# A hybrid decoder trunk on one core: output weight sums moved to VectorE in quarter pieces, and an opening without GpSimd

## The chip, the cores and the metric

The kernel runs on one core of a Trainium2 chip. The metric is device time in microseconds. Three runs of the kernel before took 1044.41, 1044.99 and 1047.21 us; the median is 1044.99. The core has five engines with a queue of instructions each: TensorE (PE in the rows, PEld for its weight loads), VectorE (DVE), ScalarE (ACT), GpSimd (POOL) and SyncE (SP), which here only issues DMAs. Each engine works its queue in order.

## The reference

One layer over 1056 tokens (1024 prompt tokens and 8 samples of 4), model width 1024, all in float32:

```python
n = rmsnorm(h, g_in)
proj = n @ w_in                  # z_a | xBC (x 1024, B 256, C 256) | dt 16 | z_b | u_b
ya = ssd_branch(z_a, xbc, dt)    # causal conv (width 4) + SiLU, chunked SSD scan, gate, grouped norm
yb = s5_branch(u_b, z_b)         # diagonal complex scan, gelu, GLU, gate
h = h + concat(ya, yb) @ w_out
gate = sigmoid(rmsnorm(h, g_ple) @ w_ple_gate)
h = h + (p @ w_ple_proj) * gate
y = rmsnorm(h, g_final)
```

The outputs are y and the new convolution, SSD and S5 states.

## The kernel before

Tokens stand on the free axis in three chunks of 352 columns, channels on the 128 partitions. Every float32 product is made of three matmuls: a weight block and the activations are each split into a rounded high part (ScalarE copies it) and a low part (VectorE subtracts), and high x high, high x low and low x high are summed in PSUM. One projection tile (`dense`) is 3 chunks x 8 blocks of K x 3 = 72 matmuls.

The stages, in the order of the code:

- **Opening.** PE multiplies zeros (`zp`), then the tiles of p @ w_ple_proj (`pp_tile` 0 to 7, 18 matmuls each, inputs `p_h`, `p_l`). Beside it the input norm is made for each of the three chunks: `norm_sum` (ScalarE squares the eight blocks of x into `xsq`, seven adds collect them in `xsa`), `norm_tok` (PE sums over partitions into `nsp`; then twelve tiny VectorE instructions on 88 x 4 values, `nv`, `ny`, `nt`, make the reciprocal root), `norm_apply` (PE spreads the root to all partitions, `nrb`; VectorE scales the eight blocks of x, and each is split into `n_h` and `n_l`). The adds of chunk 0 are VectorE's, those of chunks 1 and 2 GpSimd's; of chunk 1 GpSimd also makes three of the eight `n_l`.
- **First tiles and S5 coefficients.** Tiles u0, z0 and u1 are computed chunk by chunk, and the norms of chunks 1 and 2 are put between their matmuls by the table `mids`. Then VectorE works out the S5 coefficients (`s5_coef_base`, `s5_coef_batch`) while PE does the other u tiles; PE transposes their results (`wp`).
- **Middle (`MID`).** Seventeen tiles: twelve convolution tiles (`conv_tile`: 72 matmuls, then three long VectorE instructions into `acc`), four z tiles, one small `dt` tile. Behind each tile but the first stands one of 16 S5 batches (`s5_batch`): PE makes `vr` and `vi`, VectorE turns, scans and turns back into `sst`, PE makes the output `yp` from `sst`.
- **SSD**, in 16 units, with the other z tiles among them; then the GLU, then w_out, then gate and final norm.

The product with w_out is made of 7 block products instead of 8 (Strassen's scheme). It needs four sums of weight blocks, s1 to s4. `wo_sums` makes them: for each of 4 blocks i it loads a21, a22, a11, a12 (two DMAs of 128 x 512 each) into row buffers `wa` of 1024 columns, makes four GpSimd instructions of 128 x 1024, and stores each sum to `ws_d` in DRAM. They are read there much later. The code asks for two sums behind each of `MID`'s tiles 1 to 8.

What sets the order: a scheduler of the framework lays out every engine's queue from modelled times, by readiness and by the order of the code, so an instruction may be placed well before where the code has it. `tc.issue_after` (here `behind`) makes it place an instruction after another one. Loads and stores of SP stand in one queue: a store that waits for its data holds all that is behind it. Row buffers come from one pool of 28.

Of the kernel before, what the change touches and what calls it, by code (L numbers as in the profile page):

```python
# [26 lines left out]
WSUM = {i: 2 for i in range(1, 9)}  # L27
# [5 lines left out]
V_GIN, V_CW, V_CB, V_NG, V_GLUB, V_GPLE, V_GFIN = 0, 8, 56, 68, 76, 84, 92  # L33
C_CAUS, C_ONE, C_SMASK, C_BM, C_E8, C_I32, C_SAME, C_E16, C_ID, C_N = 0, 128, 256, 288, 296, 360, 392, 424, 440, 568
# [3 lines left out]
def hymba_ssd_s5_kernel(  # L38
# [29 lines left out]
    NSUM, NSPL = (V, G, G), ((), (1, 3, 5), ())  # L68
# [95 lines left out]
    WO_SUM = ("s1", "s2", "s3", "s4")  # L164
# [7 lines left out]
    def wo_sums():  # L172

        for i in range(4):
            a = {}
            for n, o, x, y, op, ld in (("s1", "a22", "a21", "a22", ALU.add, ("a21", "a22")),
                                       ("s3", "a21", "a11", "a21", ALU.subtract, ("a11",)),
                                       ("s2", "a11", "a22", "a11", ALU.subtract, ()),
                                       ("s4", "a12", "a12", "a11", ALU.subtract, ("a12",))):
                for blk in ld:  # L180
                    a[blk] = row("wa")[:, 0:1024]
                    for q, src in enumerate(wo_src(blk, i)):
                        dma(out=a[blk][:, 512 * q:512 * q + 512], in_=src)
                tt(a[o], a[x], a[y], op, G)
                dma(out=ws_d[WO_SUM.index(n), i], in_=a[o])
                yield
# [29 lines left out]
    def dense(w, rows_h, rows_l, evac, K=8, ko=0, chunks=((0, CW), (CW, CW), (2 * CW, CW)), ps_of=lambda c: psd_(),  # L216
              after=None, mid=None):
        hi, lo = w
        chained = after is not None
        for c, (t0, n) in enumerate(chunks):  # L220
            ps = ps_of(c)[:, 0:n]
            i = 0
            for k in range(K):
                if mid and k == mid[0]:
                    pe_end[0] = after
                    mid[1]()
                    after = pe_end[0]
# [23 lines left out]
    pe_end, v_end = [None], [None]  # L251
# [82 lines left out]
    for i in range(8):  # L334
        pe_end[0] = PE.matmul(out=zp[:, 0:128], lhsT=z0, rhs=z0, start=True, stop=True)
# [17 lines left out]
    def pp_tile(m, w):  # L353
        o = pet("pe", F32) if m in PEP else cvt("pe")

        def evac(c, t0, n, ps):
            if c == 1:
                ts(o[:, t0:t0 + n], ps, 0.5, None, ALU.mult)
            else:
                act(o[:, t0:t0 + n], ps, scale=0.5)  # L360
        pe_end[0] = dense(w, p_h, p_l, evac, K=2, ko=2 * (m % 4), ps_of=lambda c: psb("psd") if c == 2 else psd_(),
                          after=pe_end[0])
        dms(out=pp_d[m], in_=o[:, 0:T])

    def norm_sum(c):
# [3 lines left out]
        for k in range(1, 8):  # L369
            sq = ev("xsq")  # L370
            act(sq, x[k], AF.Square)
            add(sa, sa, sq, NSUM[c])
# [5 lines left out]
    def norm_apply(c, y):  # L378
        x = [xr[k][:, c * CW:c * CW + CW] for k in range(8)]
        rs = rstd_bcast(y, pe_end[0])  # L380
        for k in range(8):
            stt(x[k], x[k], vc[:, V_GIN + k:V_GIN + k + 1], rs, ALU.mult, ALU.mult)
            end = split(n_h[k][:, c * CW:c * CW + CW], n_l[k][:, c * CW:c * CW + CW], x[k],
                        G if k in NSPL[c] else V)
# [9 lines left out]
    n_end = norm_apply(0, y0)  # L394
# [3 lines left out]
    sa1 = norm_sum(1)  # L398
    pp_tile(4, w_pp2)
    pp_tile(5, w_pp2)  # L400
    w_u0 = split_w(r_u0)
    y1 = norm_tok(sa1)
    pp_tile(6, w_pp2)
    pp_tile(7, w_pp2)
    with behind(n_end):
        w_z0 = split_w(r_z0, [row(n, F32R)[:, 0:1024] for n in ("zwh", "zwl")])
    w_u1 = load_w(M_U + 1)
# [214 lines left out]
    def conv_tile(m, name):  # L622
# [16 lines left out]
        for k in (2, 1, 0):  # L639
            stt(acc[:, 0:1080], raw[:, k:k + 1080], cw(k), acc[:, 0:1080], ALU.mult, ALU.add)  # L640
# [81 lines left out]
    def z_evac(j):  # L722
        dst = zb_d[j] if j < 8 else za_d[j - 8]

        def evac(c, t0, n, ps):
            t = ev("zt", n)
            if j >= 8:
                act(t, ps, AF.Tanh, scale=0.5)
                stt(t, t, 1.0, ps, ALU.add, ALU.mult)
# [4 lines left out]
            for a, b, d0, ns in ((0, nn, 0, 8),) + (((nn, n, NPT, 4),) if nn < n else ()):  # L734
# [3 lines left out]
                stt(v, v, 1.0, pv, ALU.add, ALU.mult)  # L738
# [283 lines left out]
    later = {}  # L1022

    def norm2():
        later["y"] = norm_tok(norm_sum(2))

    def norm_end():
        later["end"] = norm_apply(2, later["y"])

    mids = {(0, 0): (3, lambda: norm_apply(1, y1)), (0, 1): (0, norm2), (1, 0): (0, norm_end)}  # L1030
    for c in range(3):
        for i, (w, e) in enumerate(first):
            pe_end[0] = dense(w, n_h, n_l, lambda _, t0, n, ps: e(c, t0, n, ps), chunks=((CW * c, CW),), after=pe_end[0],
                              mid=mids.get((c, i)))
    n_end = later["end"]
# [13 lines left out]
    nb, sums = 0, wo_sums()  # L1049
    for i, nm in enumerate(MID):  # L1050
# [345 lines left out]
```

## Time and profile before

| | |
|---|---|
| Median of 3 runs | 1044.99 us |
| The profiled execution | 1044.09 us, its span 1042.3 us |
| PE busy | 995.8 us (96% of the span) |
| DVE busy | 814.2 us (78%) |
| ACT busy | 454.4 us (44%) |
| POOL busy | 222.5 us (21%) |

The profile gives for one execution the start and duration of every instruction, what ended an engine's idle time, and PE's granted clock. PE is the engine that is nearly always busy. So the time moves with PE's idle stretches, with the stretches in which its clock is granted at half (1.2 instead of 2.4 GHz), and with the number of its matmuls. Matmuls overlap: what one costs is the distance from its start to the next start, not its duration. The same holds for VectorE's instructions.

### The profile page before, as it was taken

To read this page: it belongs to the slowest core of one execution; us is meant where nothing else is said; L and a number is where in the kernel's file an instruction comes from. 1 tells how busy PE (TensorE), PEld (TensorE's weight loads), DVE (VectorE), ACT (ScalarE), POOL (GpSimd) and SP (SyncE) were. 2 spreads that over 40 slices of the span, in tenths; PEclk is the share of its full clock that TensorE was granted. 3 is DMA by queue.
4 is the path that set the end of the run, shared out by engine and by line. 5 is a ranking of instruction groups with operands and counts; after the bars stand their busy time and mean duration, and the time that the engine had idled before them with its cause. 6 is when DMAs were issued, how large, how long until landed. Compare 5 with 4: busy or idle time off the path is not lost.

```text
span 1042.3 us, 19520 instructions
## 1 busy us (share of the span) xinstructions
PE 995.8 (96%) x7148; PEld 942.8 (90%) x7148; DVE 814.2 (78%) x1804; ACT 454.4 (44%) x1006; POOL 222.5 (21%) x215
## 2 busy tenths in 40 slices
PE   7999999997899999999999998899999999899995
PEld 6999989986799999999878887799999999899995
DVE  5888999776989887873866777868688879977466
ACT  6532233344245353445764445244345445454221
POOL 2401030025500000001243323121232015541221
PEclk8899999998999999999999999999999999999998
DMA  9426599886855644545456667576544323335122
GB/s 343 162 67 200 154 275 259 210 276 247 240 187 153 196 113 129 168 141 151 132 180 199 201 191 214 161 208 166 166 120 134 110 88 118 112 124 171 48 94 104
DMA packets 170832, 174.88 MB, mean 168 GB/s; under 512 B 47728, under 2 KB 129136, under 8 KB 170736
## 3 DMA queue, kind: packets, MB, share of 16 engines
q1 hardware_dynamic: 140704, 153.23, 48.6%
q10 hardware_dynamic: 30032, 20.40, 6.2%
q8 instruction: 56, 0.92, 0.4%
q14 instruction: 40, 0.33, 0.1%
HBM read 123.05 MB, written 54.73 MB: 171 GB/s over the span
## 4 chain that ended last, share of the span: by engine, by line
PE 67%; DVE 17%; DMA 7%; issue 4%; ACT 3%; SPq 0%; POOL 0%; DVEq 0%; ACTq 0%
PE psd L231 43%; PE psd L1204 12%; PE yp L306 3%; DVE wl L77 2%; DVE rb L77 2%; PE nrb L290 1%; DVE acc L89 1%; DMA gr<-gd 1%; PE yd L860 1%; DMA ab<-acs_d 1%; PE st L912 1%; ACT ab L74 1%; DVE x L89 1%; ACT wh L74 1%; DVE opn L77 1%
## 5 line engine op out<-in xcount | busy, mean ns | idle before, releaser
L231 PE MATMUL psd<-n_h,wh 128*128 128x352 f32 x840 | 275.1, 327 | 0.0
L231 PE MATMUL psd<-n_l,wh 128*128 128x352 f32 x840 | 274.5, 327 | 0.0
L231 PE MATMUL psd<-n_h,wl 128*128 128x352 f32 x840 | 273.8, 326 | 0.0
L231 PEld LDWEIGHTS psd<-n_h,wh 128*128 128x128 f32 x840 | 158.1, 188 | 10.0 <-issue 9.8
L1204 PE MATMUL psd<-opn,wh 128*128 128x264 f32 x896 | 164.0, 285 | 0.0
L231 PEld LDWEIGHTS psd<-n_h,wl 128*128 128x128 f32 x840 | 158.3, 188 | 3.1 <-issue 2.6
L231 PEld LDWEIGHTS psd<-n_l,wh 128*128 128x128 f32 x840 | 158.2, 188 | 2.8 <-issue 2.5
L1204 PEld LDWEIGHTS psd<-opn,wh 128*128 128x128 f32 x896 | 138.6, 188 | 0.1
L1204 PE MATMUL psd<-opn,wl 128*128 128x264 f32 x448 | 126.9, 285 | 3.6 <-DVE wl L77 3.6
L74 ACT ACTIVATE wh<-wr 128x512 fp32r<-128x512 f32 x147 | 85.7, 623 | 94.3 <-PE psd L231 38.1
L77 DVE TENSOR_TENSOR wl<-wr,wh 128x512 fp32r<-128x512 f32 x146 | 106.9, 758 | 24.4 <-ACT wh L74 23.5
L1204 PEld LDWEIGHTS psd<-opn,wl 128*128 128x128 f32 x448 | 84.2, 188 | 4.2 <-DVE wl L77 4.2
L77 POOL TENSOR_TENSOR wa<-wa 128x1024 f32<-128x1024 f32 x16 | 44.2, 2761 | 121.7 <-DMA wa<-wall 111.3
L74 ACT ACTIVATE ab<-ab,tok 128x128 f32<-128x128 f32 (+1 forms) x144 | 42.8, 379 | 53.3 <-DMA ab<-acs_d 40.7
L231 PE MATMUL psd<-g_h,wh 128*128 128x384 f32 (+1 forms) x168 | 54.1, 322 | 0.1
L231 PE MATMUL psd<-g_l,wh 128*128 128x384 f32 (+1 forms) x168 | 54.0, 321 | 0.0
L231 PE MATMUL psd<-g_h,wl 128*128 128x384 f32 (+1 forms) x168 | 53.9, 321 | 0.0
L77 POOL TENSOR_TENSOR xl<-xl,h 128x264 f32<-128x264 f32 x32 | 29.7, 933 | 87.9 <-DVE h L77 34.7
L231 PE MATMUL psd<-hg_h,gwl 128*128 128x400 f32 (+1 forms) x144 | 46.6, 324 | 0.0
L231 PE MATMUL psd<-hg_h,gwh 128*128 128x400 f32 (+1 forms) x144 | 46.5, 323 | 0.0
L231 PE MATMUL psd<-hg_l,gwh 128*128 128x400 f32 (+1 forms) x144 | 46.4, 323 | 0.0
L74 ACT ACT_TABLE_LOAD x29 | 37.2, 1283 | 19.2 <-DVE acc L89 11.1
(323 smaller groups left out, 2079.0 us busy)
## 6 DMA issues: line engine op xcount, KB each, us to landing
wr<-wall SPq DMA_DIRECT2D x128, 256.0 KB, 3.4
wa<-wall SPq DMA_DIRECT2D x32, 256.0 KB, 6.1
ws_d<-wa SPq DMA_DIRECT2D x16, 512.0 KB, 5.5
mm<-md SPq DMA_DIRECT2D x16, 512.0 KB, 5.3
ab<-acs_d SPq DMA_DIRECT2D x16, 512.0 KB, 5.2
wr<-ws_d SPq DMA_DIRECT2D x32, 256.0 KB, 2.9
ud<-ub ACTq DMA_DIRECT2D x8, 576.0 KB, 4.7
u<-ud SPq DMA_DIRECT2D x16, 288.0 KB, 4.1
```

The costliest lines, as they stand in the source:

```text
L74: return S.activation(out=out, in_=in_, func=func, **kw)
L77: return (eng or V).tensor_tensor(out=out, in0=a, in1=b, op=op)
L89: return V.scalar_tensor_tensor(out=out, in0=a, scalar=s, in1=b, op0=op0, op1=op1)
L231: end = PE.matmul(out=ps, lhsT=a[:, ko + k, :], rhs=b, start=(i == 0), stop=(i == 3 * K - 1))
L290: end = PE.matmul(out=rb[:, qt * j:qt * j + qt], lhsT=y[:, j:j + 1].to_broadcast([qt, 128]), rhs=ident[0:qt, 0:qt], start=True, stop=True)
L306: self.last = f(*a, **kw)
L860: PE.matmul(out=yd[64 * (e % 2):64 * (e % 2) + 64, e // 2], lhsT=x1[:, e], rhs=mt[:, e], start=True, stop=True)
L912: PE.matmul(out=st, lhsT=bk, rhs=x2.rearrange("p e q -> p (e q)"), start=True, stop=True)
L1204: PE.matmul(out=ps, lhsT=a[:, k, :], rhs=b, start=(k == 0 and q == 0), stop=(k == 7 and q == 2))
```

## The change

- **Sums.** `wo_sums(n)` now works on a quarter: 256 columns of each of the four blocks in one row buffer, loaded by two DMAs (128 x 2 x 256, so pieces of 1 KB where they were 2 KB), four VectorE instructions of 128 x 256 in place, one store of 512 KB in pieces of 1 KB. There are 16 such quarters, so 64 VectorE instructions in place of 16 GpSimd ones. Each is placed behind the last long VectorE instruction (`v_mid`) of its tile, at tiles 4 to 13 of `MID`, one or two a tile.
- **Opening.** All adds and all `n_l` are VectorE's; GpSimd has no part in it. The adds of chunk 1 are placed behind the root of chunk 0 and ahead of its scalings, those of chunk 2 behind the root of chunk 1 and ahead of its scalings. `mids` puts the norms later between the first tiles: chunk 1 is scaled behind u0 of chunk 0 (before: inside it), chunk 2 behind u0 of chunk 1 (before: ahead of it). VectorE's part in emptying PSUM of pp tiles 4 to 7 goes to ScalarE.
- **Zeros.** One more zero product at the start, and 4, 8 and 2 between the first matmuls of pp tile 0 (`ZER`).

```diff
@@ -26,3 +26,3 @@
 HT, CQ = 528, 264
-WSUM = {i: 2 for i in range(1, 9)}
+WSUM = {4: 1, 5: 2, 6: 1, 7: 2, 8: 1, 9: 2, 10: 2, 11: 2, 12: 2, 13: 1}
 PCH = ((0, 384), (384, 384), (768, 288))
@@ -33,2 +33,3 @@
 V_GIN, V_CW, V_CB, V_NG, V_GLUB, V_GPLE, V_GFIN = 0, 8, 56, 68, 76, 84, 92
+ZER = {(0, 1): 4, (1, 0): 8, (1, 1): 2}
 C_CAUS, C_ONE, C_SMASK, C_BM, C_E8, C_I32, C_SAME, C_E16, C_ID, C_N = 0, 128, 256, 288, 296, 360, 392, 424, 440, 568
@@ -67,3 +68,3 @@
     V, S, G, PE = nc.vector, nc.scalar, nc.gpsimd, nc.tensor
-    NSUM, NSPL = (V, G, G), ((), (1, 3, 5), ())
+    
 
@@ -163,3 +164,3 @@
     WO_BLK = dict(a11=(0, 0), a12=(0, 512), a21=(4, 0), a22=(4, 512))
-    WO_SUM = ("s1", "s2", "s3", "s4")
+    WO_SUM = ("s2", "s4", "s3", "s1")
 
@@ -171,17 +172,15 @@
 
-    def wo_sums():
+    def wo_sums(n):
 
-        for i in range(4):
-            a = {}
-            for n, o, x, y, op, ld in (("s1", "a22", "a21", "a22", ALU.add, ("a21", "a22")),
-                                       ("s3", "a21", "a11", "a21", ALU.subtract, ("a11",)),
-                                       ("s2", "a11", "a22", "a11", ALU.subtract, ()),
-                                       ("s4", "a12", "a12", "a11", ALU.subtract, ("a12",))):
-                for blk in ld:
-                    a[blk] = row("wa")[:, 0:1024]
-                    for q, src in enumerate(wo_src(blk, i)):
-                        dma(out=a[blk][:, 512 * q:512 * q + 512], in_=src)
-                tt(a[o], a[x], a[y], op, G)
-                dma(out=ws_d[WO_SUM.index(n), i], in_=a[o])
-                yield
+        i, q = n // 4, n % 4
+        base, o = (M_WOA, M_WOB)[q // 2] + i, 256 * (q % 2)
+        a = row("wa")[:, 0:1024].rearrange("p (m h c) -> p m h c", m=2, h=2)
+        for m in range(2):
+            dma(out=a[:, m], in_=wall[base + 4 * m].rearrange("p (h c) -> p h c", h=2)[:, :, o:o + 256])
+        a11, a12, a21, a22 = (a[:, j // 2, j % 2] for j in range(4))
+        add(a22, a21, a22)
+        sub(a21, a11, a21)
+        sub(a11, a22, a11)
+        sub(a12, a12, a11)
+        dma(out=ws_d[:, i, :, 256 * q:256 * q + 256].rearrange("s p c -> p s c"), in_=a.rearrange("p m h c -> p (m h) c"))
 
@@ -216,3 +215,3 @@
     def dense(w, rows_h, rows_l, evac, K=8, ko=0, chunks=((0, CW), (CW, CW), (2 * CW, CW)), ps_of=lambda c: psd_(),
-              after=None, mid=None):
+              after=None, mid=()):
         hi, lo = w
@@ -223,6 +222,7 @@
             for k in range(K):
-                if mid and k == mid[0]:
-                    pe_end[0] = after
-                    mid[1]()
-                    after = pe_end[0]
+                for k_, f in mid:
+                    if (c, k) == k_ if isinstance(k_, tuple) else k == k_:
+                        pe_end[0] = after
+                        f()
+                        after = pe_end[0]
                 h, l = rows_h[k][:, t0:t0 + n], rows_l[k][:, t0:t0 + n]
...
@@ -333,4 +333,9 @@
     zp = psa("zp")
-    for i in range(8):
-        pe_end[0] = PE.matmul(out=zp[:, 0:128], lhsT=z0, rhs=z0, start=True, stop=True)
+
+    def zeros(n):
+        for _ in range(n):
+            with behind(pe_end[0]):
+                pe_end[0] = PE.matmul(out=zp[:, 0:128], lhsT=z0, rhs=z0, start=True, stop=True)
+
+    zeros(9)
     for (t0, t1), (a, b) in zip(PS, WS):
@@ -356,3 +361,3 @@
         def evac(c, t0, n, ps):
-            if c == 1:
+            if c == 1 and m < 4:
                 ts(o[:, t0:t0 + n], ps, 0.5, None, ALU.mult)
@@ -361,3 +366,3 @@
         pe_end[0] = dense(w, p_h, p_l, evac, K=2, ko=2 * (m % 4), ps_of=lambda c: psb("psd") if c == 2 else psd_(),
-                          after=pe_end[0])
+                          after=pe_end[0], mid=[(q, lambda n=n: zeros(n)) for q, n in ZER.items()] if m == 0 else ())
         dms(out=pp_d[m], in_=o[:, 0:T])
@@ -371,3 +376,3 @@
             act(sq, x[k], AF.Square)
-            add(sa, sa, sq, NSUM[c])
+            s_end[0] = add(sa, sa, sq)
         return sa
@@ -382,4 +387,3 @@
             stt(x[k], x[k], vc[:, V_GIN + k:V_GIN + k + 1], rs, ALU.mult, ALU.mult)
-            end = split(n_h[k][:, c * CW:c * CW + CW], n_l[k][:, c * CW:c * CW + CW], x[k],
-                        G if k in NSPL[c] else V)
+            end = split(n_h[k][:, c * CW:c * CW + CW], n_l[k][:, c * CW:c * CW + CW], x[k])
         return end
@@ -393,3 +397,6 @@
     pp_tile(3, w_pp)
-    n_end = norm_apply(0, y0)
+    with behind(v_end[0]):
+        sa1 = norm_sum(1)
+    with behind(s_end[0]):
+        n_end = [norm_apply(0, y0)]
     r_z0 = load_raw(M_ZB)
@@ -397,12 +404,12 @@
         dma(out=xr[k][:, 2 * CW:T], in_=xT[k, :, 2 * CW:T])
-    sa1 = norm_sum(1)
     pp_tile(4, w_pp2)
-    pp_tile(5, w_pp2)
-    w_u0 = split_w(r_u0)
     y1 = norm_tok(sa1)
-    pp_tile(6, w_pp2)
-    pp_tile(7, w_pp2)
-    with behind(n_end):
+    for m in range(5, 8):
+        pp_tile(m, w_pp2)
+    with behind(n_end[0]):
+        w_u0 = split_w(r_u0)
         w_z0 = split_w(r_z0, [row(n, F32R)[:, 0:1024] for n in ("zwh", "zwl")])
-    w_u1 = load_w(M_U + 1)
+        with behind(v_end[0]):
+            sa2 = norm_sum(2)
+        w_u1 = load_w(M_U + 1)
     pe_es.close()
@@ -639,3 +646,3 @@
         for k in (2, 1, 0):
-            stt(acc[:, 0:1080], raw[:, k:k + 1080], cw(k), acc[:, 0:1080], ALU.mult, ALU.add)
+            v_mid[0] = stt(acc[:, 0:1080], raw[:, k:k + 1080], cw(k), acc[:, 0:1080], ALU.mult, ALU.add)
         act(cso[:, m, 0:3], raw[:, 1024:1027])
@@ -728,3 +735,3 @@
                 act(t, ps, AF.Tanh, scale=0.5)
-                stt(t, t, 1.0, ps, ALU.add, ALU.mult)
+                v_mid[0] = stt(t, t, 1.0, ps, ALU.add, ALU.mult)
                 dma(out=dst[:, t0:t0 + n], in_=t)
...
@@ -1021,11 +1028,14 @@
     first = ((w_u0, u_tile(0)), (w_z0, z_evac(0)), (w_u1, u_tile(1)))
-    later = {}
+    ny = {1: y1}
 
-    def norm2():
-        later["y"] = norm_tok(norm_sum(2))
+    def norm_a():
+        ny[2] = norm_tok(sa2)
 
-    def norm_end():
-        later["end"] = norm_apply(2, later["y"])
+    def norm_b(c):
+        def f():
+            with behind(s_end[0] if c == 1 else None):
+                n_end.append(norm_apply(c, ny[c]))
+        return f
 
-    mids = {(0, 0): (3, lambda: norm_apply(1, y1)), (0, 1): (0, norm2), (1, 0): (0, norm_end)}
+    mids = {(0, 1): [(0, norm_b(1))], (0, 2): [(1, norm_a)], (1, 1): [(0, norm_b(2))]}
     for c in range(3):
@@ -1033,4 +1043,4 @@
             pe_end[0] = dense(w, n_h, n_l, lambda _, t0, n, ps: e(c, t0, n, ps), chunks=((CW * c, CW),), after=pe_end[0],
-                              mid=mids.get((c, i)))
-    n_end = later["end"]
+                              mid=mids.get((c, i), ()))
+    n_end = n_end[2]
     with tc.issue_after(n_end.ins):
@@ -1048,3 +1058,3 @@
     s5c_["p1"] = pool("s51", 1, s5_es)
-    nb, sums = 0, wo_sums()
+    nb = nw = 0
     for i, nm in enumerate(MID):
@@ -1056,2 +1066,6 @@
             {"b": bt, "c": ct, "x": xs}[nm[0]][int(nm[1])] = conv_tile(CONV[nm], nm)
+        for _ in range(WSUM.get(i, 0)):
+            with behind(v_mid[0]):
+                wo_sums(nw)
+            nw += 1
         if i > 0 and nb < 16:
@@ -1059,4 +1073,2 @@
             nb += 1
-        for _ in range(WSUM.get(i, 0)):
-            next(sums)
     dma(out=o_conv, in_=cso)
...
```

Three places show how the queues change. First VectorE in the opening, from the end of chunk 0's root (`ny`) on; `wl` is the low part of a weight, `x_100` to `x_107` are the blocks of x. Before:

```order
L77 TENSOR_TENSOR nt<-nv,ny 88x4
L89 SCALAR_TENSOR_TENSOR nt<-ny,nt 88x4
L89 SCALAR_TENSOR_TENSOR ny<-nt,ny 88x4
L77 TENSOR_TENSOR wl<-wr,wh 128x512
L89 SCALAR_TENSOR_TENSOR x_100<-x_100,vc,nrb 128x352
```

And in the changed kernel, the same place in VectorE's queue:

```order
L78 TENSOR_TENSOR nt<-nv,ny 88x4
L90 SCALAR_TENSOR_TENSOR nt<-ny,nt 88x4
L90 SCALAR_TENSOR_TENSOR ny<-nt,ny 88x4
L78 TENSOR_TENSOR xsa<-xsa,xsq 128x352 x7
L90 SCALAR_TENSOR_TENSOR x_100<-x_100,vc,nrb 128x352
```

Seven adds of chunk 1 now stand between the root and the scalings; the weight's split has gone behind them.

Second, VectorE in a convolution tile of `MID` (tile 5, x1) in the changed kernel; `acc` is the convolution, `ta`, `tb`, `ur`, `ui` and `sst` are S5, `wa` the sums:

```order
L90 SCALAR_TENSOR_TENSOR acc<-x_3358,vc,acc 128x1080
L78 TENSOR_TENSOR wa<-wa 128x256 x2
L78 TENSOR_TENSOR sr<-sst 128x256
L78 TENSOR_TENSOR ta<-vi,cr 128x256
L78 TENSOR_TENSOR tb<-vr,sr 128x256
L78 TENSOR_TENSOR a4h<-a4h,vr 128x16
L78 TENSOR_TENSOR a4h<-a4h,vi 128x16
L822 SCALAR_TENSOR_TENSOR ur<-mag_609,ur 128x128 x2
L78 TENSOR_TENSOR wa<-wa 128x256 x2
L78 TENSOR_TENSOR ui<-ta,tb 128x256
L78 TENSOR_TENSOR wa<-wa 128x256 x2
```

Before, no sum stood in VectorE's queue; eight (two quarters) now stand among this tile's S5 work.

Third, PE at the end of the middle: `yp` is the output of the last S5 batch, `cb` and `xt` the first step of SSD, `psd` the matmuls of a z tile. Before:

```order
L231 MATMUL psd<-n_h_117,wl 128x352
L303 MATMUL yp<-sst,om 128x136
L306 MATMUL yp<-sst,om 128x136 x7
L306 MATMUL yp<-u_5373,mm 128x136 x4
L891 MATMUL cb<-c_2642,b_2541 128x128
L892 MATMUL cb<-ident_r,b_2541 128x128
```

And in the changed kernel:

```order
L231 MATMUL psd<-n_h_117,wl 128x352
L303 MATMUL yp<-sst,om 128x136
L306 MATMUL yp<-sst,om 128x136 x7
L306 MATMUL yp<-u_5436,mm 128x136 x4
L231 MATMUL psd<-n_h_110,wh 128x352
L231 MATMUL psd<-n_l_118,wh 128x352
```

The last `yp` stands 72 matmuls of z tiles behind the last convolution tile before, 120 in the changed kernel; the first `cb` and `xt` have gone ahead of it, and the first output of SSD (`yd`) comes 50 z matmuls later than before.

## Rows read from the trace of the kernel before

**Rows 1.** The page, part 1: busy time of each engine

```profile
PE 995.8 (96%) x7148; PEld 942.8 (90%) x7148; DVE 814.2 (78%) x1804; ACT 454.4 (44%) x1006; POOL 222.5 (21%) x215
```

**Rows 2.** Timeline of PE: start, us, instruction, count, idle time before it and releaser

```profile
0.99 3.78 PE L335 MATMUL zp<-zero 128*128 128x128 f32 x16 [0.99 <-POOL zero L332]
...
19.74 0.72 PE L268 MATMUL nsp<-cs,xsa 128*88 128x1 f32 x8
26.73 2.01 PE L290 MATMUL nrb<-ident_r,ny 88*128 88x88 f32 x8 [3.28 <-DVE ny L89]
...
37.30 0.32 PE L231 MATMUL psd<-p_l,wh 128*128 128x352 f32 x1
37.46 0.32 PE L231 MATMUL psd<-p_h,wl 128*128 128x352 f32 x1
...
44.95 1.12 PE L290 MATMUL nrb<-ident_r,ny 88*128 88x88 f32 x8 [0.94 <-DVE ny L89]
...
145.35 0.33 PE L303 MATMUL wp<-ident_r,wt 128*128 128x128 f32 x1 [2.17 <-DVE wt L77]
...
242.43 0.59 PE L303 MATMUL yp<-sst,om 64*128 64x136 f32 x1 [7.02 <-DVE sst L77]
...
281.14 0.41 PE L303 MATMUL yp<-sst,om 64*128 64x136 f32 x1 [4.92 <-DVE sst L77]
```

**Rows 3.** Windows: stretch, length, busy us of each engine, PE clock, DMA share, GB/s

```profile
300.00:480.00 180.00, 179.83 (x1354) 170.35 (x1353) 149.71 (x364) 86.97 (x180) 0.00 (x0) 1.00 0.49 143
480.00:500.00 20.00, 18.48 (x126) 17.51 (x125) 6.19 (x11) 13.42 (x37) 4.58 (x12) 1.00 0.49 139
...
8.00:16.00 8.00, 7.13 (x25) 6.58 (x26) 5.84 (x10) 6.21 (x14) 0.36 (x4) 0.57 1.05 386
26.00:32.00 6.00, 5.27 (x20) 5.27 (x21) 4.50 (x9) 1.90 (x5) 1.13 (x2) 0.50 0.39 141
240.00:248.00 8.00, 5.57 (x32) 5.32 (x32) 4.88 (x10) 4.84 (x7) 1.16 (x1) 0.55 0.60 174
280.00:288.00 8.00, 6.86 (x44) 6.62 (x45) 7.93 (x23) 2.73 (x6) 3.21 (x2) 0.79 0.75 224
```

**Rows 4.** Timeline of DVE in the opening

```profile
20.69 0.75 DVE L93 TENSOR_SCALAR ny<-nv 88x4 int32<-88x4 int32 x1
...
28.78 4.03 DVE L89 SCALAR_TENSOR_TENSOR x<-x,vc,nrb 128x352 f32<-128x352 f32 x8 [1.50 <-PE nrb L290]
...
54.54 0.16 DVE L93 TENSOR_SCALAR ny<-nv 88x4 int32<-88x4 int32 x1
...
62.09 3.56 DVE L77 TENSOR_TENSOR n_l<-x,n_h 128x352 fp32r<-128x352 f32 x8
```

**Rows 5.** Timeline of POOL

```profile
19.45 6.07 POOL L77 TENSOR_TENSOR xsa<-xsa,xsq 128x352 f32<-128x352 f32 x6 [8.75 <-ACT xsq L74]
...
230.92 10.24 POOL L77 TENSOR_TENSOR wa<-wa 128x1024 f32<-128x1024 f32 x4 [1.68 <-DMA wa<-wall]
```

**Rows 6.** Timeline of DVE in the middle

```profile
236.52 2.44 DVE L77 TENSOR_TENSOR ta<-ui,cr 128x256 f32<-128x256 f32 x1
238.88 2.56 DVE L77 TENSOR_TENSOR tb<-ur,sr 128x256 f32<-128x256 f32 x1
...
281.40 0.41 DVE L77 TENSOR_TENSOR ta<-vr,cr 128x256 f32<-128x256 f32 x1
281.74 0.41 DVE L77 TENSOR_TENSOR tb<-vi,sr 128x256 f32<-128x256 f32 x1
```

**Rows 7.** Instructions that write `wa`: shortest, median, longest ns; first and last start

```profile
L77 POOL TENSOR_TENSOR wa<-wa x16: 2402/2569/5372, 96.2 to 280.9; 128x1024 f32<-128x1024 f32 x16
```

**Rows 8.** Waits of DVE from 300 to 480 us

```profile
DVE tb L77 <- PE vi L306: 12.9, 9, 1.9
DVE sst L77 <- PE yp L306: 8.5, 3, 4.2
```

**Rows 9.** Waits of SP's queue

```profile
SPq L185 <- POOL wa L77: 8.9, 2, 8.3
```

More of the change, by code (lines that the diff above doesn't have):

```diff
@@ L250, in hymba_ssd_s5_kernel @@
     nw_p = pool("nw", bufs=2)
-    pe_end, v_end = [None], [None]
+    pe_end, v_end, v_mid, s_end = [None], [None], [None], [None]
     def rstd(sqs, n):
@@ L737, in evac @@
                 act(v, pv, AF.Tanh, scale=0.5)
-                stt(v, v, 1.0, pv, ALU.add, ALU.mult)
+                v_mid[0] = stt(v, v, 1.0, pv, ALU.add, ALU.mult)
                 o = dst[:, 0:NPT] if d0 == 0 else dst[:, NPT:T]
@@ L1085, in hymba_ssd_s5_kernel @@
             z_next()
-    assert nz[0] == 16
+    assert nz[0] == 16 and nw == 16
     glb = const.tile([128, 8], F32, name="glb")
```

## The prediction

> **What bounds the kernel now.** I began with the page's busy times: PE works 96% of the span, no other engine more than 78% [rows 1]. So I looked for what PE loses: in its timeline the starts that carry an idle time and its releaser [rows 2], and in the table of windows the stretches with a low granted clock [rows 3]. Two places matter. In the opening PE waits 3.28 us and 0.94 us for a reciprocal root of VectorE. In the middle it waits 7.02 and 4.92 us for `sst` of an S5 batch, and once, at 145 us, 2.17 us for a coefficient [rows 2]. Around them the clock is low: 0.57 from 8 to 16 us, 0.50 from 26 to 32, 0.55 from 240 to 248, 0.79 from 280 to 288; from 300 to 480 it is 1.00 and PE is busy for 179.83 of 180 us [rows 3].
>
> Then I asked why VectorE is late there. A root's instruction on 88 values (`ny<-nv`) takes 0.75 us at 20.69 and 0.16 at 54.54 [rows 4]; at 20.69 GpSimd is in a run of six adds from 19.45 to 25.5 [rows 5]. In the middle a 128 x 256 instruction takes 2.44 and 2.56 us at 236.52 and 238.88, and 0.41 at 281.40 [rows 6]; from 230.92 to 241.16 GpSimd is in a run of four sums [rows 5]. The long one costs about as much as one sum of GpSimd, whose median is 2.57 us [rows 7]. So GpSimd's work on row buffers holds VectorE up, and PE waits for VectorE. The change takes exactly this work off GpSimd.
>
> **The change part by part.** All sums are against the profiled execution: 1044.09 us, of which 1042.3 is the span and 1.8 lies around it; the median of the runs is 0.9 above it.
>
> *The sixteen sums leave GpSimd.* Four in a row stand between VectorE and the wait at 242.43; the stretched instructions are over 2 us longer each, so without them `sst` is some 8 us earlier, more than the 7.02 that PE waits [rows 2, 6]. What was late next is then PE itself. The wait goes: -7.0. The clock behind it: 5.57 busy us at 0.55 would be 45% shorter, -2.5 [rows 3]. At 281.14 the same: five stretched instructions between 257 and 281, 4.92 us of wait, -4.9, and 6.86 busy us at 0.79, -1.4 [rows 2, 3]. At 145.35 PE waits 2.17 us; three of the sums were run early, the first at 96.2 [rows 7], and VectorE, whose coefficients are its longest chain there, gets back about 2.2 us for each, and starts the chain earlier (below): -2.2. Together -18.0. Bounds: -8 (VectorE has a second cause of delay at both places and half stays) and -18.
>
> *The same sums come to VectorE.* 64 instructions of 128 x 256. Two of that form start 0.34 us apart where nothing holds them [rows 6], so 64 x 0.34 = 21.8 us, in ten tiles. The cover is VectorE's idle time: 180 - 149.7 = 30.3 us between 300 and 480 us [rows 3], over thirteen batches, 2.3 a tile, against 2.2 that come to it. Of this idle time 21.4 us were waits for PE's `vi` and `yp` [rows 8], thus time in which VectorE was ahead. On average it just fits. Between 480 and 500 VectorE is busy for only 6.19 of 20 us [rows 3], so that a lag can be worked off there. A convolution tile with two quarters overfills, a z tile makes room. Ends: 0 (all hidden) and 21.8 (none). I take 4, nearer to 0, since the row for VectorE's idle time is the larger one. If the cover is gone, what waits is the next `yp` on PE, and `wl`, the next tile's weight.
>
> The Trainium skill (Perfetto Trace Analysis, section Optimizing Scalar/DVE Operations) says that with a saturated VectorE moving elementwise work to GpSimd may make sense, though the two share a port so that it might not help. By its first half the change goes the wrong way, and 21.8 us would be added for nothing; by its second half the sums cost VectorE time wherever they run. The rows bear out the second half: 16 x about 2 us held up against 21.8 us of own work.
>
> *The S5 batches end later in PE's queue.* The last `yp` moves 48 matmuls back and SSD's first output 50; at 0.16 us from start to start [rows 2] that is 8 us of z matmuls that no longer lie between the steps of SSD's first half. Ends 0 and 8; I take 1, since VectorE's load falls to 6.19 of 20 us where SSD begins, and the late batches use that [rows 3].
>
> *Loads and stores of the sums.* As many DMAs as before (32 and 16), as many bytes, smaller pieces. The store now waits for VectorE in SP's queue, and the next tile's weights and the next batch's inputs stand behind it. Before, SP waited twice for a sum, at most 8.3 us, 8.9 in all [rows 9]. A weight is loaded about one tile (11.5 us of matmuls) ahead, so I take 0 and keep 0 to 10 as bounds.
>
> *The opening.* Its first part: from 8 to 16 us the clock is 0.57 [rows 3]; at full clock the 8 us would be some 3.4 shorter. Fourteen zero products stand against this between the first matmuls, at full clock some 0.24 us each (an estimate: half of what one of the first eight takes, 3.78 us / 8 [rows 2]), 3.4, of which 1.9 lie in gaps that PE has there anyway: net -1.9, and `nsp` comes at 17.8 instead of 19.74 [rows 2]. If the clock falls all the same: +1.5. Second, the root: twelve instructions at 0.16 to 0.2 us [rows 4] are 2.3 us, where they took 6 (from `ny` at 20.69 to `nrb` at 26.73); PE does tile 3 meanwhile (18 matmuls, 2.9 us): the wait of 3.28 falls to 0.3, -3.0. Third, 26 to 32 us at clock 0.50 [rows 3]: -2.5. Fourth, the wait of 0.94 at 44.95: -0.9. Together -8.3.
>
> Against this VectorE gets 14 adds and 3 `n_l`; eight `n_l` of that form take 3.56 us, 0.44 each [rows 4], so 17 x 0.44 = 7.5 us more. But it no longer loses some 4 us in the root and some 3 to 4 in its work beside GpSimd's second run of adds. Is it in time? The root ends near 21.0; seven adds 3.1, eight scalings 4.03, eight `n_l` 3.56 [rows 4], the weight of u0 1.2: 32.9. PE, from its `nrb` near 22.3, has 72 matmuls of pp tiles 4 to 7, 11.5 us, and a second `nsp`, 0.6: 34.4. It fits with 1.5 us to spare. Later PE has 24 matmuls (u0) ahead of each scaling, so that it is not late there either. By this walk the third `nrb` stands at 51.7 with 24 matmuls more done than before, the last `n_l` ends near 60.4, not 65.6 [rows 4], so the coefficients start 5 us earlier. I take -8.3; ends -10 and 0.
>
> Sum: -18.0 - 8.3 + 4 + 1 = -21.3, so 1022.8 for the profiled execution, 1023.7 against the median. **Forecast: 1023.7 us.**
>
> **The rivals.**
>
> *VectorE becomes the bound of ten tiles.* Its idle time is not one it can fill: it waits for PE's `vi`, and then PE for it. For: 83% busy before from 300 to 480 [rows 3], over 95% with the sums. Against: PE never waited there, and the surplus can move to the z tiles. Price: 12 to 21.8 instead of 4, so 1031 to 1041.
>
> *The opening gives nothing.* VectorE's 7.5 us come just when PE needs `n_l`; the slack is 1.5 us. For: a scaling or a weight that comes 2 us later than in the walk is already too late. Against: the walk itself, in which every term but the slack has a row. Price 8.3: 1032.
>
> *The change doesn't do what it says.* If the long instructions had another cause than GpSimd (the DMA engines' share is 0.60 and 0.75 there [rows 3]), the waits of the middle stay and VectorE has 21.8 us more. Against: the tenfold root comes and goes with GpSimd's runs. Of the opening's gain and of that at 145 us I count half, 5, and half of 21.8 against it: 1050 at worst, about 1045 with some of it hidden, no change.
>
> *SP's queue holds the loads (slower).* Sixteen stores, each behind the last sum of its quarter on VectorE; behind each the weight or the S5 inputs of the next tile. It decides from 21.3 / 16 = 1.33 us that reach PE for each store. For: the one long hold of 8.3 us before [rows 9], and VectorE nearly full. Against: loads are about a tile ahead. At 2.5 us each: 40 - 21.3 + 1045, about 1064.
>
> **How the numbers follow.** Forecast 0.60 (its own range 1014 to 1031), VectorE as the bound 0.20, the opening 0.10, no effect of GpSimd 0.04, SP 0.06. The range 1012 to 1037 holds the forecast's case, the opening's and over half of VectorE's, some 0.8. A measurement here tells 0.3% (3 us) from no change. Faster: 0.60 + 0.20 + 0.10 = 0.90; within: 0.04; slower: 0.06.
>
> **What would show it.** No VectorE instruction of 128 x 256 over 1 us before 480 us; PE without a wait for `sst` near 230 and 270 and clock 1.00 there; the first `nrb` near 21 us with clock 1.00 from 10 us on; about 22 us of `wa` on VectorE. It would be wrong if PE waits for `yp` or a weight between 290 and 450 us by more than some 10 us, if the first tile of n waits for `n_l` or `wl`, or if SSD's first half has PE idle.

## The result, and the profile after

The changed kernel took 1032.16 us in the median of four runs (1029.08 to 1034.11), the kernel before 1046.10 in four (1044.41 to 1048.22): ratio 0.9863, interval 0.9828 to 0.9898. A second set gave 0.9877 (0.9842 to 0.9911). So it is faster, by 13 to 14 us, inside the range (1012 to 1037); the forecast was 21.3. The profiled execution took 1033.53 us, its span 1031.5: 10.8 less than before.

Busy times, answering to [rows 1]; GpSimd lost 63.5 us, VectorE 10 although it now makes the sums:

```profile
PE 996.8 (97%) x7178; PEld 944.2 (92%) x7178; DVE 804.1 (78%) x1881; ACT 453.6 (44%) x1008; POOL 159.0 (15%) x182
```

PE's timeline at the places of [rows 2], with the waits that are new:

```profile
19.95 0.72 PE L268 MATMUL nsp<-cs,xsa 128*88 128x1 f32 x8
23.76 1.12 PE L290 MATMUL nrb<-ident_r,ny 88*128 88x88 f32 x8
...
41.26 1.02 PE L290 MATMUL nrb<-ident_r,ny 88*128 88x88 f32 x8
...
51.27 0.47 PE L231 MATMUL psd<-n_h,wl 128*128 128x352 f32 x1 [1.86 <-DVE wl L78]
58.33 1.02 PE L290 MATMUL nrb<-ident_r,ny 88*128 88x88 f32 x8
...
143.41 0.27 PE L303 MATMUL wp<-ident_r,wt 128*128 128x128 f32 x1
...
214.63 0.30 PE L303 MATMUL vi<-u,mm 128*64 128x136 f32 x1 [1.78 <-issue]
216.57 0.34 PE L672 MATMUL psd<-n_h,wh 128*32 128x352 f32 x1 [0.79 <-DVE wh L78]
229.72 0.38 PE L303 MATMUL yp<-sst,om 64*128 64x136 f32 x1
...
276.80 0.49 PE L303 MATMUL vi<-u,mm 128*64 128x136 f32 x1 [2.71 <-DMA mm<-md]
```

The waits for the first two roots, for the coefficient at 145 and the two long ones for `sst` are gone. In their place PE waits for a weight at 51.27, for its first S5 input (`vi`) at 214.63, for the weight of the `dt` tile, and for `mm`, the input of an S5 batch, at 276.80. The windows of [rows 3], and three more:

```profile
8.00:16.00 8.00, 8.00 (x52) 8.00 (x51) 6.75 (x12) 6.64 (x15) 0.36 (x4) 1.00 1.06 389
26.00:32.00 6.00, 5.72 (x41) 5.46 (x40) 5.69 (x14) 5.79 (x16) 0.00 (x0) 1.00 0.45 182
50.00:56.00 6.00, 4.74 (x20) 4.74 (x21) 5.86 (x18) 2.16 (x6) 0.00 (x0) 0.72 0.51 145
...
240.00:248.00 8.00, 8.00 (x53) 7.56 (x52) 3.88 (x7) 5.85 (x15) 0.46 (x1) 1.00 0.19 66
276.00:282.00 6.00, 5.20 (x32) 4.84 (x33) 3.73 (x8) 0.69 (x2) 0.00 (x0) 0.72 0.78 303
280.00:288.00 8.00, 8.00 (x51) 8.00 (x50) 8.00 (x23) 3.52 (x6) 0.00 (x0) 0.99 0.10 32
300.00:480.00 180.00, 176.70 (x1313) 168.17 (x1312) 155.62 (x401) 78.53 (x169) 2.94 (x8) 1.00 0.72 205
480.00:500.00 20.00, 20.00 (x142) 17.88 (x141) 10.37 (x20) 17.94 (x52) 3.63 (x6) 1.00 0.44 124
```

VectorE is 86% busy between 300 and 480 us, where 95% was expected, and the clock is low behind two of the new waits. In the first window the clock needs care: the trace has no clock record before 10.57 us, and the profile shows a stretch without a record as 1.00. The matmuls of 8.95 to 9.53 us still stand 0.29 us apart, which is the lower rate; from 13 us on they stand 0.16 apart. The sums on VectorE (instructions by form), and the waits of SP's queue that answer to [rows 9]:

```profile
L78 DVE TENSOR_TENSOR wa<-wa 128x256 f32<-128x256 f32 x64 | 24.9, 418 | 0.0
```

```profile
SPq L179 <- DMA ws_d<-wa: 17.7, 9, 5.2
SPq L185 <- DVE wa L78: 9.2, 6, 2.5
```

In the first line, nine times a load of the next quarter (`wa`) waited until the store of an earlier one had landed, since it takes over its buffer, and what stood behind it waited too. What that costs depends on what stands there. SP's queue before the wait at 276.80 (start, duration of the issue):

```profile
263.92 0.37 SPq L185 DMA_DIRECT2D ws_d<-wa  x1
267.52 1.22 SPq L179 DMA_DIRECT2D wa<-wall  x2
268.84 0.54 SPq L788 DMA_DIRECT2D om<-od  x1
269.48 0.38 SPq L783 DMA_DIRECT2D u<-ud  x1
269.91 0.42 SPq L785 DMA_DIRECT2D mm<-md  x1
```

The loads of `wa` start 3.6 us behind the store, and `mm` stands behind them.

### The profile page after: what moved, and what is told of

It reads as the page before. It is cut to its first block, busy times and chain, and to the rows that moved or that the text cites. A ratio compares the mean times of both kernels' runs of the same rounds, so it can differ in the third digit from the quotient of the medians.

```text
span 1031.5 us, 19570 instructions
## 1 busy us (share of the span) xinstructions
PE 996.8 (97%) x7178; PEld 944.2 (92%) x7178; DVE 804.1 (78%) x1881; ACT 453.6 (44%) x1008; POOL 159.0 (15%) x182
## 4 chain that ended last, share of the span: by engine, by line
PE 54%; DVE 8%; DMA 8%; issue 2%; ACT 2%; POOL 1%; SPq 1%; DVEq 0%; ACTq 0%; POOLq 0%
PE psd L231 32%; PE psd L1216 11%; DMA mm<-md 2%; DMA wr<-wall 2%; PE yd L867 1%; PE yp L306 1%; DMA gr<-gd 1%; PE st L919 1%; PE yo L916 1%; PE nrb L290 1%; DVE acc L90 1%; DMA xl<-xT 1%; DVE wl L78 1%; DMA ws_d<-wa 1%; DVE wa L78 1%
## 5 line engine op out<-in xcount | busy, mean ns | idle before, releaser
L78 DVE TENSOR_TENSOR wl<-wr,wh 128x512 fp32r<-128x512 f32 x146 | 104.9, 743 | 37.7 <-ACT wh L75 32.2
L90 DVE SCALAR_TENSOR_TENSOR zt<-zt,psd 128x352 f32<-128x352 f32 (+2 forms) x56 | 26.0, 464 | 18.0 <-ACT zt L75 17.8
```

Source lines behind the costliest of these rows:

```text
L78: return (eng or V).tensor_tensor(out=out, in0=a, in1=b, op=op)
L90: return V.scalar_tensor_tensor(out=out, in0=a, scalar=s, in1=b, op0=op0, op1=op1)
```

## The experiments

Each ran in five rounds beside the kernel before; ratios are to it.

**The opening alone.** `wo_sums`, `WSUM` and their call are those of before, the rest is the changed kernel.

```diff
-WSUM = {4: 1, 5: 2, 6: 1, 7: 2, 8: 1, 9: 2, 10: 2, 11: 2, 12: 2, 13: 1}
+WSUM = {i: 2 for i in range(1, 9)}
...
+                tt(a[o], a[x], a[y], op, G)
```

> Only the opening is changed (with its zero products); the sums stay on GpSimd as before. Theory: the two parts act apart, and the opening is worth what PE has gained by the end of the first tiles, some 3 us: about 1042.5 against 1046 for the kernel before. Rival: VectorE's chain of S5 coefficients does not start earlier (the third nrb of the changed kernel came at 58.2 us, before at 57.0), so PE gives the 3 us back as longer waits at 145 and 242 us: 1045 to 1046, and the wait for sst near 240 is over 8 us.

0.9908 (0.9880 to 0.9937), some 9.6 us: more than either expected. It shortens the waits that the sums were to remove: 0.47 us at 143 where there were 2.17, and 4.01 (now for `dw`) and 4.17 where there were 7.02 and 4.92.

```profile
245.40 1.99 PE L708 MATMUL ap<-dw,cs 128*128 128x128 f32 x10 [4.01 <-DVE dw L78]
276.05 0.38 PE L305 MATMUL yp<-sst,om 64*128 64x136 f32 x1 [4.17 <-DVE sst L78]
```

**The sums alone,** in two sets of runs; the opening is that of before.

```diff
-WSUM = {i: 2 for i in range(1, 9)}
+WSUM = {4: 1, 5: 2, 6: 1, 7: 2, 8: 1, 9: 2, 10: 2, 11: 2, 12: 2, 13: 1}
...
+        for _ in range(WSUM.get(i, 0)):
+            with behind(v_mid[0]):
+                wo_sums(nw)
```

> Only the sums are changed (VectorE, quarter pieces, behind the long instruction of a tile); the opening is that of before. Theory: the waits at 145, 242 and 281 us and the half clock behind two of them go (18 us), and new waits for the S5 inputs cost some 7: about 1035, that is 11 below before. Rival (the opening carries most of the gain by letting VectorE start earlier): 1040 or more, and a wait for sst of over 3 us is left near 230 to 290 us.

> The kernel before with only the sums changed, once more, beside the two versions below. Theory: the opening adds nothing to the sums, since its gain ends at the first vi: PE comes there sooner, but VectorE's coefficients and the load of mm behind them do not, and PE waits 1.7 us for it and 0.8 for the weight of the dt tile (213 to 214.6 us in the changed kernel, 214.6 in the kernel with the sums alone, without a wait). Then this kernel is again at 0.983 to 0.988, no slower than the changed one. Rival (the parts add up, the first measurement was a lucky one): 0.990 or more, that is 1037.

0.9828 (0.9795 to 0.9860) and 0.9847 (0.9825 to 0.9870), 18 and 16 us: more than the 11 expected, and no less than the whole change. So the opening adds nothing to the sums, though alone it is worth 9.6. In the second profile PE comes to the first `vi` at 214.9 without a wait, and SP issues `mm` ahead of the loads of `wa`:

```profile
262.63 0.37 SPq L184 DMA_DIRECT2D ws_d<-wa  x1
263.20 0.35 SPq L774 DMA_DIRECT2D u<-ud  x1
263.60 1.01 SPq L776 DMA_DIRECT2D mm<-md  x1
...
268.33 1.21 SPq L178 DMA_DIRECT2D wa<-wall  x2
```

Nothing in the source of the sums differs; the queue was laid out in another order, by a scheduler whose modelled times move with the opening (no run separates that cause).

PE's first matmul of the `dt` tile shows how little of the opening's gain is left there. Before, in the opening alone, and in the two profiles of the sums alone:

```profile
221.03 0.35 PE L665 MATMUL psd<-n_h,wh 128*32 128x352 f32 x1 [0.74 <-DVE wh L77]
```

```profile
216.04 0.50 PE L674 MATMUL psd<-n_h,wh 128*32 128x352 f32 x1 [0.72 <-DVE wh L78]
```

```profile
217.66 0.35 PE L663 MATMUL psd<-n_h,wh 128*32 128x352 f32 x1 [1.92 <-DVE wh L77]
```

```profile
216.22 0.35 PE L663 MATMUL psd<-n_h,wh 128*32 128x352 f32 x1 [0.20 <-DVE wh L77]
```

With both parts it starts at 216.57, and at 214.91 in the second profile of the changed kernel (next). So up to here the opening alone gains 5.0 us, the sums alone 3.4 and 4.8, and both together only 4.5 and 6.1.

**The changed kernel again.**

> The changed kernel once more, for a direct comparison with the runs beside it. Expected: the ratio 0.986 as before (some 14 us below the kernel before). In its profile the last yp comes some 4 us before that of the kernel before, and PE waits for mm by 4 to 6 us in all between 270 and 420; if those waits were of one execution only they are gone here.

0.9877. The waits are not of one execution: 1.73 us at the first `vi`, 3.04 for `mm` at 277.02, 2.88 at 370.39. The clock is low behind the first two, but not behind the third:

```profile
212.00:222.00 10.00, 8.24 (x51) 5.41 (x52) 8.21 (x23) 3.30 (x12) 0.00 (x0) 0.83 0.77 244
274.00:282.00 8.00, 4.98 (x26) 4.63 (x27) 5.17 (x10) 1.28 (x4) 0.00 (x0) 0.65 0.83 318
...
370.00:376.00 6.00, 5.61 (x44) 5.46 (x45) 3.85 (x10) 2.01 (x6) 0.00 (x0) 1.00 1.12 229
```

In the second window PE loses 3.0 us idle and 4.98 x 0.35 = 1.7 to the clock; in the first 1.8 and 1.4.

**The sums' DMAs in GpSimd's queue.**

```diff
-            dma(out=a[:, m], in_=wall[base + 4 * m]...
+            nc.gpsimd.dma_start(out=a[:, m], in_=wall[base + 4 * m]...
...
-        dma(out=ws_d[:, i, :, 256 * q:256 * q + 256]...
+        nc.gpsimd.dma_start(out=ws_d[:, i, :, 256 * q:256 * q + 256]...
```

> The changed kernel with the 32 loads and 16 stores of the sums issued by GpSimd's queue instead of SP's; the same bytes, the same VectorE work. Theory (queue): in SP's queue a store waits for VectorE and a load of the next quarter for the store to land (17.7 us in nine waits), and the S5 inputs stand behind them; off that queue PE's waits for mm (5.1 us, the longest 2.7) fall under 1 us and the time by 4 to 6, to some 1027. Rival (bandwidth): the DMA engines' share is 0.70 to 1.01 between 320 and 440 us, so the inputs land as late from any queue: waits for mm stay at 4 us or more, 1031 to 1033. Second rival: GpSimd's issuing holds VectorE up as its sums did: VectorE instructions of 128x256 over 1 us, 1035 or more.

> The kernel before with the sums on VectorE in quarter pieces and their loads and stores in GpSimd's queue. Theory: as the kernel with the sums alone, less its waits for mm (1.7 us in its profile): 1027 to 1030. Rival (with DMAs issued by GpSimd something behind the middle gets slower, as the product with w_out did in the one profile of the changed kernel with that queue, 177.2 us against 171.8 to 172.4): 1032 or more, and the product with w_out takes over 175 us again.

With the changed opening 0.9864 (0.9839 to 0.9890), with the old one 0.9876 (0.9857 to 0.9895). With the changed opening the waits for `mm` fall to 1.3 us, nearly as the queue's theory has it, though DMA share stays at 0.71 between 300 and 480, so bandwidth did not hold them up. With the old opening they do not fall: 1.9 us, where the first profile of the sums alone has 1.7. The time does not follow in either. At the first `vi` and the `dt` tile PE now loses 3.35 and 0.72 us; with the old opening 3.28 at the `dt` tile. The product with w_out took 177.2 and 173.1 us, and 176.7 in the version with three mends below (171.6 to 172.9 in the kernels with the sums on VectorE and SP's queue); in the two long ones its granted clock was 0.98 and 0.97. These places make up for it; why they come with that queue was not separated.

**Own buffer for the raw weight of z0.**

```diff
-    r_z0 = load_raw(M_ZB)
+    rz = row("rz")[:, 0:1024]
+    dma(out=rz, in_=wall[M_ZB])
+    r_z0 = [rz[:, 0:512], rz[:, 512:1024]]
```

> The changed kernel with the raw weight of z0 loaded in one piece into a free row buffer, so that it waits for no wr buffer. Theory: the two wr buffers are held by u0's weight until its split, which now stands behind the scalings and n_l of chunk 0; so z0's and u1's loads were issued at 36 to 48 us, VectorE waited 2.8 us for them and PE 1.86 at 51.3, and the clock fell behind it (1.5 us). With an own buffer the wait and the clock loss go: about 3 less, some 1029, and the third nrb comes near 55 instead of 58.2. Rival: VectorE's own work for chunk 1 (seven adds, eight scalings, eight n_l, 11 us) is what is late, and PE waits for nrb or n_l instead: no change, 1032.

0.9863 (0.9838 to 0.9889). The cause of the wait at 51 is confirmed, the gain is not: that wait is gone (1.03 for `nrb` in its place), the third `nrb` comes at 54.6 us and the first `vi` at 211.1, 3.5 us sooner, of which this execution was 1.3 ahead at `nsp` already (18.64 against 19.95). But the `vi` is waited for all the same (1.91), and PE waits 2.94 for `mm` at 275: the next places took it.

**No zero products between the matmuls.**

```diff
-ZER = {(0, 1): 4, (1, 0): 8, (1, 1): 2}
+ZER = {}
...
-    zeros(9)
+    zeros(8)
```

> The changed kernel without the fourteen zero products between the first matmuls of pp tile 0 and with eight at the start. My prediction's term: the zeros are worth 1.9 us, so this kernel is 2 slower. What the trace of the changed kernel says instead: ten of them (8 and 2) cost 2.56 us of PE, and the sixteen matmuls behind them ran 0.135 us shorter each, 2.2 us, so nsp did not come earlier (19.95 against 19.74): no difference, within 1 us. Third: without them the half clock lasts into the root of chunk 0 and the time is 3 or more above.

0.9837 (0.9807 to 0.9868), the first n matmul at 36.8 us. In the three kernels of the changed opening without these zeros it comes at 36.8 to 38.0, in the profiles with them at 36.1 to 37.7: they bring nothing that shows there. They do raise the rate sooner: the clock record begins, at full, at 4.1 to 10.6 us with them and at 13.9 to 15.8 without; but, as the expectation counts, they cost PE about as much as that gives back. That the median is 4 us below the changed kernel's beside it is not the opening's doing by its trace, and the intervals overlap; its waits at the first `vi` and near 273 are shorter (0.82 and 1.83).

**Quarter sums on GpSimd, one VectorE instruction of four.**

```diff
-        add(a22, a21, a22)
+        add(a22, a21, a22, G)
...
```

> The changed kernel with the same 64 quarter instructions at the same places, but on GpSimd. Theory (GpSimd's work on row buffers holds VectorE up whenever it runs): 64 instructions of about 0.65 us (a quarter of 2.57) stretch VectorE's instructions beside them, now in the tiles where VectorE is 95% busy or more; the 42 us of GpSimd's time come to VectorE in place of 21.8: PE waits for sst return by 15 us or more, 1045 or more. Rival (only the four sums in a row ahead of 242 and 281 us mattered, the place and not the engine): as the changed kernel or 3 us better, since VectorE has 21.8 us less to do, 1029 to 1033.

0.9933 (0.9910 to 0.9955): 6 us worse than the changed kernel, between both expectations. GpSimd still holds VectorE up, but by a quarter piece only, and PE's waits for `sst` are back: 8.2 us in three, where 15 or more were expected.

```profile
280.74 0.56 PE L303 MATMUL yp<-sst,om 64*128 64x136 f32 x1 [4.97 <-DVE sst L78]
```

VectorE's instructions by form from 240 to 300 us, first here, then in the changed kernel:

```profile
L78 DVE TENSOR_TENSOR sst<-r,r 128x256 f32<-128x256 f32 x8 | 5.2, 684 | 0.7 <-PE yp L306 0.6
L78 DVE TENSOR_TENSOR tb<-ui,sr 128x256 f32<-128x256 f32 x3 | 2.3, 775 | 0.0
```

```profile
L78 DVE TENSOR_TENSOR sst<-r,r 128x256 f32<-128x256 f32 x10 | 3.8, 418 | 0.0
L78 DVE TENSOR_TENSOR tb<-ui,sr 128x256 f32<-128x256 f32 x3 | 1.3, 419 | 0.0
```

The other way round, with less on VectorE (three of the four sums are left out):

```diff
         add(a22, a21, a22)
-        sub(a21, a11, a21)
-        sub(a11, a22, a11)
-        sub(a12, a12, a11)
```

> The changed kernel with one VectorE instruction of each quarter instead of four: 48 instructions of 0.34 us, 16.3 us of VectorE's time, are left out (so three of the four sums are not made); loads, stores and places stay. Rival of the prediction (VectorE is the bound of the ten tiles): 8 to 16 us faster than the changed kernel. Theory (VectorE's idle time covers the sums; what is left are the loads behind SP's queue): PE's waits between 290 and 480 us that end with VectorE are under 1 us already, so the time stays within 2 us of the changed kernel's and the waits for mm stay.

0.9888 (0.9857 to 0.9920), no faster than the changed kernel. Much of the 16 us went into VectorE's idle time: its wait for `vi` rose from 3.3 to 12.8 us between 300 and 480. It is not a clean subtraction, since the queues were laid out anew here too: PE waits 4.3 us for `yp` after 320 us, where the changed kernel waits 0.85, and the profile names no releaser for those waits.

**The mends together.** Both versions: no zeros between the matmuls, own buffer for z0; the first with the sums' DMAs in GpSimd's queue, the second in SP's.

> The changed kernel with three mends: no zero products between the matmuls of pp tile 0 (eight at the start), the raw weight of z0 in its own row buffer, loads and stores of the sums in GpSimd's queue. Theory (three separate costs): the coefficients end 3 us sooner and so does the first vi (211 instead of 213 to 214.6), the waits for mm (4 to 7 us) go, so 5 to 8 below the changed kernel: 1026 to 1029. Rival (what one place gives back the next one takes: VectorE is 91% busy or more from 290 to 380 us and sets the S5 batches): not below the changed kernel by more than 3, 1031 or more.

> The version with three mends, but with the loads and stores of the sums in SP's queue again (no zero products between the matmuls, raw z0 in its own buffer stay). In this version's SP queue the first mm load behind a store stands ahead of the next two wa loads, where in the changed kernel the wa loads, which wait for the store to land, stand ahead of it. Theory (what counts in SP's queue is whether the S5 inputs stand behind a wa load that waits for a store): no wait of over 2 us for mm near 270, and the time as with three mends or up to 3 above, 1025 to 1029, ratio 0.980 to 0.983. Rival (the queue as such costs, any order): waits for mm of 4 us or more again, 1030 or more.

0.9799 (0.9780 to 0.9817), 1025.30 us, and 0.9768 (0.9733 to 0.9802), 1025.61 us: better than the changed kernel and than before, beyond their intervals; better than the sums alone in one of its two sets, while the interval of the other (0.9795 to 0.9860) overlaps. The second's queue, and its window near 277:

```profile
258.60 0.37 SPq L185 DMA_DIRECT2D ws_d<-wa  x1
259.18 0.34 SPq L785 DMA_DIRECT2D u<-ud  x1
259.57 1.03 SPq L787 DMA_DIRECT2D mm<-md  x1
...
264.29 1.21 SPq L179 DMA_DIRECT2D wa<-wall  x2
```

```profile
274.00:282.00 8.00, 8.00 (x59) 7.59 (x58) 8.00 (x17) 2.96 (x4) 0.00 (x0) 1.00 0.15 44
```

`mm` stands ahead of the loads that wait for the store, PE does not wait there, and the first `vi` (210.9) has no wait either. The loads of `wa` wait for the stores as long as in the changed kernel (17.7), here and in the second profile of the sums alone, where PE does not wait near 277 either:

```profile
SPq L179 <- DMA ws_d<-wa: 17.4, 9, 4.3
```

```profile
SPq L178 <- DMA ws_d<-wa: 21.9, 9, 5.8
```

So at 277 it is the order in SP's queue that costs, not the queue and not the length of its waits. The two waits, over the kernels with the sums on VectorE:

| kernel | us at first `vi` and `dt` | us for `vi`, 260 to 290 | PE idle, 300 us to the last `yp` | ratio |
|---|---|---|---|---|
| changed, two profiles | 2.57, 2.50 | 2.71, 3.04 | 3.3, 5.3 | 0.9863, 0.9877 |
| z0 in its own buffer | 2.75 | 2.94 | 3.2 | 0.9863 |
| one add of four | 2.65 | 1.64 | 6.3 | 0.9888 |
| GpSimd's queue | 4.07 | 0 | 2.2 | 0.9864 |
| GpSimd's queue, old opening | 3.28 | 0 | 1.9 | 0.9876 |
| no zeros | 1.65 | 1.83 | 3.9 | 0.9837 |
| sums alone, two profiles | 1.92, 0.20 | 0, 0 | 3.9, 3.6 | 0.9828, 0.9847 |
| three mends | 1.49 | 0 | 3.0 | 0.9799 |
| two mends, SP's queue | 0.17 | 0 | 4.8 | 0.9768 |

Kernels that lose over 3.2 us at the two places lie at 0.9837 to 0.9888, those that lose under 2 at 0.9768 to 0.9847. PE's idle time behind 300 us does not go with the ratio. The two places were picked after the runs, and each profile is one execution, so the table is a sign and no proof.

## Why the prediction was right, and where it fell short

The time, 1032.16 us, lies in the range but just above the forecast's own case (1014 to 1031), at the price that I gave the rival "the opening gives nothing" (1032). The number alone can't tell them apart; the runs do, part by part.

**The sums leave GpSimd (-18.0): right.** No 128 x 256 instruction of VectorE takes over 1 us between 216 and 480, PE does not wait for `sst` near 230 or 281, the clock is 1.00 from 240 to 248. With the quarter sums put back on GpSimd the stretching comes back. What I called a tenfold root was less: 0.75 us against 0.16 for one instruction, and 6 us against some 3 for the whole.

**VectorE's 21.8 us (+4): right in kind, too dear.** PE's waits for `yp` between 205 and 480 us are 0.85 in all, and leaving out 16.3 us of the work gains nothing. The rival of VectorE as the bound falls, as far as that run can tell. The first half of the rule weighed in the prediction (the Trainium skill, Perfetto Trace Analysis, section Optimizing Scalar/DVE Operations), by which it may make sense to hand work of a saturated VectorE to GpSimd, was no guide here: VectorE was 86% busy, and with the quarters on GpSimd the kernel is 6 us slower.

**SSD's cover (+1): about right.** PE loses 1.3 us between the last `yp` and the first GLU product; before 1.8, in the second profile 2.2. The two profiles leave no cost to be seen.

**Loads and stores on SP (0): wrong size.** I looked at the store's wait for VectorE (9.2 us, as the 8.9 before) and at weights a tile ahead. I did not see that the next load of `wa` takes over a buffer whose store has not landed, and holds the S5 inputs if they stand behind it: 5.1 us of waits for `mm`, and with the clock behind the wait at 277 4.2 and 4.7 us there alone, in the two profiles.

**The opening (-8.3): its steps held in part.** The root was right: 3.81 us from `nsp` to `nrb`, where it was 6.99, and the clock 1.00 from 26 to 32. The zeros were not: taken as -1.9, they give nothing (`nsp` at 19.95, predicted 17.8), and so the first `nrb` came at 23.8, not near 21. The weight was not: I counted VectorE's instructions up to 60.4 us, but not that u0's raw weight, split behind the scalings now, keeps both `wr` buffers, so that SP issues z0's weight at 36 us and u1's at 41 and 45; ScalarE and VectorE wait for them, the last split of u1's weight misses its turn and stands behind eight scalings (46.60 to 50.53), and PE waits at 51.27. SP's queue in the changed kernel:

```profile
36.23 1.31 SPq L160 DMA_DIRECT2D wr<-wall  x2
...
41.33 0.33 SPq L160 DMA_DIRECT2D wr<-wall  x1
...
44.80 0.53 SPq L160 DMA_DIRECT2D wr<-wall  x1
```

With 16% of the n matmuls done PE is 3.3 us ahead of before, 4.9 in the second profile. The third `nrb`, predicted at 51.7, came at 58.3 and 56.1, the last `n_l` ended at 67.3 and 65.2 instead of 60.4, so the coefficients did not start 5 us earlier but 1.1 later (first `wp`) and 0.5 earlier.

**The sum: the step that failed.** Alone, each part was worth its term or more: 9.6 (8.3 predicted) and 16 to 18 (13). I added them. But they shorten the same waits: the opening alone took 1.7 + 3.0 + 0.75 us off those at 145, 242 and 281, which the sums remove whole. And PE, now early, meets a chain that is not: last `wp` on PE (199.0), `kd`, eight loads of `md`, `mm` issued at 208.5 and landed at 214.4, first `vi` at 214.6. (The profile names no releaser for that wait; that it is `mm` is read from the landing.) The three versions with z0's own buffer have the chain sooner, `mm` issued near 204.9 and landed at 210.1 to 211.0: PE, there at 209.2 and 209.3, still waited 1.91 and 0.89 us in two of them, and in the third, there at 210.9, not at all. So at the `dt` tile both parts together have gained 5.3 us in the mean of two profiles, where 5.0 and 4.1 alone make 9.1: 3.8 are gone. Of these 1.7 are the wait at 145; the other 2.1 I put down to this chain.

In all: 26 less 5.4 of overlap, 2.1 at the chain and 4.2 to 4.7 at 277 is some 14, against 13 to 14 measured. That it fits so closely is partly luck: two profiles of the same kernel differ by 1.4 and 1.7 us at the `dt` tile, and the intervals are 5 to 7 us wide.

## What to carry to other kernels

Gains that are worked out part by part add up only where the parts shorten different waits, and where what PE meets next is early too: follow each gain to the next place at which another chain hands over, and ask what sets it. Where an edit moves loads and stores into a queue, write down for each of them which buffer it takes over and when that comes free, for a load that waits for a store's landing holds all behind it, and what is urgent must stand ahead of it. And a part that gains alone may undo another's order in a scheduled queue, so the parts are tried one by one, too.

## What the runs showed of the hardware that I had not expected

- The hold-up of VectorE goes with the size of GpSimd's piece: beside 128 x 1024 sums (2.57 us) its 128 x 256 instructions took 2.44 and 2.56 us, beside 128 x 256 sums (0.89 us) 0.68 and 0.78 in the mean of two forms and 0.96 at most, and 0.42 alone.
- A short wait of PE can cost more than half as much again in the clock, or nothing: after 3.04 us idle the granted clock was 0.65 over 274 to 282 (its lower level is 0.50), 1.7 us; after 2.88 us at 370.39 in the same execution it stayed at 1.00.
- At the start PE can be at half rate while the granted clock reads as full, because there is no record yet: without the zeros the windows from 4 to 16 us say 1.00, but the trace's first clock record stands at 13.89, and the matmuls stood 0.29 us apart until 13.64 and 0.16 from 13.92 on.

```profile
13.35 0.49 PE L231 MATMUL psd<-p_h,wh 128*128 128x352 f32 x1
13.64 0.45 PE L231 MATMUL psd<-p_l,wh 128*128 128x352 f32 x1
13.92 0.32 PE L231 MATMUL psd<-p_h,wl 128*128 128x352 f32 x1
14.08 0.32 PE L231 MATMUL psd<-p_h,wh 128*128 128x352 f32 x1
```
